# Token operands of the block products formed beside two plain tiles, reloads issued from GpSimd, raw tiles in two rings

## The chip, the cores and the metric

The kernel runs on one core of a Trainium2 chip. A core has a matrix engine (TensorE, PE in the rows), a vector engine (VectorE, DVE), a scalar engine (ScalarE, ACT), GpSimd (POOL) and SyncE (SP). Each runs its own instructions strictly in its own order, and they wait for one another by semaphores. SP and POOL here do little but issue DMAs. The metric is the device time of one launch in microseconds, lower is better.

## The reference

One step of a streaming encoder with two layers over 576 tokens: 512 frames of a new stream and 64 frames of a running one, 2048 features, 16 heads. Each layer is a gated token mixer with a residual. Layer A mixes by chunk-band attention, layer B by latent attention, in which queries come from a low-rank latent `cq` and have a plain part of 128 columns for each head and a rotary part of 64.

```python
def a_prompt(x, ln, w_in, g_q, g_k, table, w_out):
    q, k, v, g = a_project(rmsnorm(x, ln), w_in, g_q, g_k)
...
    y = x + (jax.nn.silu(g) * o) @ w_out

def b_project(h, pos, w_in, g_qa, w_uq, g_kva, g_qn, g_qr, g_kr):
    cq, ckv, kr, g = jnp.split(h @ w_in, [B_Q_RANK, B_Q_RANK + B_KV_RANK, B_Q_RANK + B_KV_RANK + B_ROPE], axis=-1)
    q = (rmsnorm(cq, g_qa) @ w_uq).reshape(b, s, B_HEADS, B_QK)
    q_nope = rmsnorm(q[..., :B_NOPE], g_qn)
    q_rope = rope(rmsnorm(q[..., B_NOPE:], g_qr), pos)
    ckv = rmsnorm(ckv, g_kva)
    k_rope = rope(rmsnorm(kr, g_kr), pos)
    return q_nope, q_rope, ckv, k_rope, g
```

## The kernel before

Features lie on the 128 partitions and the 576 tokens along the free axis, so an activation is 16 tiles of 128x576. Weights and activations are split into a high and a low part, and a product is three matmuls (high x high, low x high, high x low) into the same PSUM tile, in two halves of 288 tokens (`mm3`). The high part is a cast on ACT (L203), the low part a subtraction on DVE (L204); together they are `split`.

The order of the matmuls is written out by a planner, the class behind `od_`: streams of work yield to it, it keeps a clock of its own, and it hands out PSUM tiles of three kinds; the kind `mm`, in which a projection accumulates, has two. PE runs this order and no other. On ACT, DVE, SP and POOL a scheduler sets the order when the kernel is built.

**Output projection, in both layers.** Of the 16 output tiles the first two (m=0, 1) are accumulated beside the last heads of the attention (`both`). Then the scope of the attention closes, and `out_a` or `out_b` runs: the residual is added to m=0 and 1 on DVE (x or by, L833 in layer A and L1222 in layer B), which frees their two `mm` tiles; m=2 and 3 are plain (`proj`, 16 steps of 6 matmuls each); the other twelve go in pairs through `block_pairs`, which makes a pair of outputs from seven half-width products. These need the token operands X of `block_operands`: for each of eight j, four subtractions on DVE and three splits (a cast on ACT and a subtraction on DVE each), on 128x288 halves; they read the gated attention outputs `o[j]` and `o[j + 8]`. In layer A these are still in memory (oA, which the rows name a0sg to a15sg); in layer B they were written to `od` in DRAM, and 16 tiles `bf` are loaded back (L1209). A fourth operand (`last`, boh and bol in layer B) is split after m=3. All of `block_operands` but `last` stands ahead of `out_a` and `out_b` in the program.

**Latents and queries of layer B.** The layer's input comes back from DRAM (`bx`, 16 loads on SP), is scaled and split. Then the latents are projected (cq, kr, ckv), and 24 projections u follow, eight times a rotary tile r and two query tiles q: r0, q0, q1, r1, q2, q3, r2 and so on. Each is accumulated in one `mm` tile and copied by ACT to an SBUF tile called raw (`raw_of`, L478), and the copy frees the `mm` tile. Beside the u the planner lets gates and the other latents through. The chain of a raw tile: square (ACT, L443), cast, sums over the partitions on PE, an inverse root (ACT), scaling on DVE (L474). A query tile is then stored to DRAM by POOL (`qd`, L989), a rotary tile goes through `rope` with four small DMAs on SP and is split (L203, L204), and the key's rotary tile krraw is stored by POOL (`krT`, L945). A tile's memory is free after the last of these. All raw tiles (bx, cqraw, krraw, r, q, ckvraw) come from one pool `latraw` of seven tiles (RAWB), each in the memory of an earlier one that is done.

Of the kernel before, what the change touches and what calls it, by code (L numbers as in the profile page):

```python
# [15 lines left out]
F32 = mybir.dt.float32  # L16
F32R = mybir.dt.float32r
# [101 lines left out]
def encoder(tc, xT, wa_in, wa_out, wb_in, wuq, wuk, wuqr, wuv, wb_out, kcT, vc, ckvcT, krcT, gains, rtab,  # L119
# [128 lines left out]
    def both(pss, name, ws, xs, before):  # L248
# [10 lines left out]
        yield from gens[1]  # L259

    def block_operands(o, o2, pool, name):

        L, R = slice(0, 288), slice(288, 576)
        X = {1: [], 2: [], 3: [], 4: [], 5: [], 6: [], 7: []}
        for j in range(8):  # L270
            X[1].append([x[:, L] for x in o2[j]])
            X[2].append([x[:, L] for x in o2[j + 8]])
            X[3].append([x[:, R] for x in o2[j + 8]])

        def put(p, j, src):
            if p == 4:
                hi, lo = [x[:, R] for x in o2[j]]
            else:
                hi = pool.tile([P, 288], F32R, tag="T", bufs=48, name=f"{name}T{p}h{j}")
                lo = pool.tile([P, 288], F32R, tag="T", bufs=48, name=f"{name}T{p}l{j}")  # L280
            split(src, hi, lo)
            X[p].append((hi, lo))

        sub = ALU.subtract
        for j in range(8):
            a, b = o[j], o[j + 8]
            V.tensor_tensor(out=a[:, L], in0=a[:, R], in1=a[:, L], op=sub)
            put(5, j, a[:, L])
            V.tensor_tensor(out=a[:, R], in0=b[:, R], in1=a[:, R], op=sub)
            V.tensor_tensor(out=b[:, R], in0=b[:, R], in1=a[:, L], op=sub)  # L290
            put(6, j, b[:, R])
            put(7, j, a[:, R])
            V.tensor_tensor(out=b[:, L], in0=b[:, L], in1=b[:, R], op=sub)

        def last():
            for j in range(8):
                put(4, j, o[j + 8][:, L])
        return X, last

# [175 lines left out]

    def raw_of(ps, tp, w, name):
        raw = tp("raw", F32, name)[:, :w]
        ACT.copy(two(raw), ps[:, :, :w // 2])  # L478
        od_.give("mm", L_M)
        return raw  # L480
# [321 lines left out]
    g_T, Tp = pool("blocksa", side="right")  # L802
    X, last_a = block_operands(oA, o2, Tp, "ao")
    g_ao, aop = pool("aout", side="right")
# [18 lines left out]
    def out_a():  # L823
        for m in range(4):
            xr = residual_a(m)
            if m < 2:
                ps = first[m]
            else:
                yield "mm"
                ps = ps_of("mm", f"ao{m}")  # L830
                yield from proj(ps, wo, o2, N)
            x1 = tpo("x1", F32, f"x1_{m}")
            V.tensor_tensor(out=two(x1), in0=ps[:, :, :288], in1=two(xr), op=ALU.add)  # L833
            od_.give("mm", L_M)
            done_a(m, x1)
        last_a()
        yield from block_pairs(wa_out, X, [(m, m + 1) for m in range(4, KT, 2)], raw_a, residual_a,
                               lambda m: tpo("x1", F32, f"x1_{m}"), done_a, "ao")
# [16 lines left out]
    g_l, lp = pool("lat")  # L855
    g_r, lrp = pool("latraw")

    def tpl(tag, dt, name):
        if tag == "raw":
            return lrp.tile([P, N], dt, tag=tag, bufs=RAWB, name=name)  # L860
        bufs = {"s1": SB, "s2": SB, "s3": S3}.get(tag, 1)
        return lp.tile([P, N], dt, tag=tag, bufs=bufs, name=name)

    h = []
    for m in range(KT):
        x1 = tpl("raw", F32, f"bx{m}")
        nc.sync.dma_start(x1, x1d[m * P:(m + 1) * P, :])
        hi = x1p.tile([P, N], F32R, tag="x1", bufs=32, name=f"bh{m}")
        lo = x1p.tile([P, N], F32R, tag="x1", bufs=32, name=f"bl{m}")
        split_g(x1, gn[:, G_LNB + m:G_LNB + m + 1], hi, lo)  # L870
        h.append((hi, lo))
# [34 lines left out]
    def q_latent(m, ps):  # L906
        raw = raw_of(ps, tpl, N, f"cqraw{m}")
        raws.append(raw)
# [14 lines left out]
    def kv_latent(m, ps):  # L923
        raw = raw_of(ps, tpl, N, f"ckvraw{m}")
        raws.append(raw)
# [13 lines left out]
    def rotary_key(ps):  # L939

        raw = raw_of(ps, tpl, N, "krraw")
        st = yield from squares(raw, tpl, N, blk, "kr")
# [41 lines left out]
    def query_chain(hd, ps):  # L984
        n_ = f"q{hd}"
        raw = raw_of(ps, tpl, N, n_ + "raw")
        st = yield from squares(raw, tpl, N, ones, n_)
# [5 lines left out]
    def rotary_chain(pr, ps):  # L993
        n_ = f"r{pr}"
        raw = raw_of(ps, tpl, N, n_ + "raw")
        st = yield from squares(raw, tpl, N, blk, n_)
# [16 lines left out]
    od_.run()  # L1013
    close(g_r)
    close(g_l)
# [189 lines left out]

    oB = []
    for kt in range(KT):
        oB.append(bo.tile([P, N], F32, tag="o", bufs=16, name=f"bf{kt}"))
        nc.sync.dma_start(oB[kt], od[kt * P:(kt + 1) * P, :])  # L1209
    X, last_b = block_operands(oB, o2, bo, "bo")  # L1210

    def out_b():
        for m in range(4):
# [3 lines left out]
            else:  # L1217
                yield "mm"
                ps = ps_of("mm", f"bo{m}")
                yield from proj(ps, wo, o2, N)  # L1220
            y = out_tile_b(m)
# [19 lines left out]
LAHEAD = 1  # L1241
RAWB, SB, S1H, S2H, S3 = 7, 4, 3, 1, 1
S1A, S2A, S3A, L_RS = 3, 2, 1, 5.0
# [83 lines left out]
```

## Time and profile before

| | |
|---|---|
| median of 3 runs | 2041.31 us (2041.11 to 2043.01) |
| profiled execution, its own time | 2043.23 us |
| its span | 2041.5 us |
| mean granted clock of TensorE | 0.991 |
| PE busy | 1990.0 us, 97% |
| DVE busy | 1350.7 us, 66% |
| ACT busy | 1103.4 us, 54% |
| POOL busy | 74.3 us, 4% |

The profile shows one execution. Its own time is 1.7 us more than its span and 1.9 us more than the median. PE is busy in nearly all of the span, so the page is read for the places where PE is idle: the list of its waits, with what released each, then the busy time by stretch, and in a stretch the timelines of the engines. The granted clock is TensorE's, 1.00 for its full speed and 0.50 for half of it.

### The profile page before, as it was taken

The page shows a single profiled execution, that of the slowest core. Times are in us where ns is not written, and L with a number is a line of the kernel's source. Part 1 is how long each engine was busy: PE and PEld are TensorE (multiplying, and loading weights), DVE is VectorE, ACT ScalarE, POOL GpSimd, SP SyncE. Part 2 cuts the span into 40 slices and gives each one's busy share as a digit, 9 for nine tenths or more (in the row PEclk, how much of TensorE's full clock was granted, in tenths as well). Part 3 has the DMA queues.
Part 4 walks back from the last instruction along what each step waited for, and adds up shares of the span by engine and source line. Part 5 has one row for each costly group of instructions (what it writes and reads, how often), then busy time and mean ns, then how long its engine had stood idle before and what let it go on. Part 6 is the DMA issues. An engine that isn't in the chain of part 4 may idle for free.

```text
span 2041.5 us, 37543 instructions
## 1 busy us (share of the span) xinstructions
PE 1990.0 (97%) x14692; PEld 1969.5 (96%) x14692; DVE 1350.7 (66%) x2651; ACT 1103.4 (54%) x2034; POOL 74.3 (4%) x141
## 2 busy tenths in 40 slices
PE   8999999999999999999999899999999999995998
PEld 8999999999999999999999899999999999995998
DVE  7665555555555555558778648887776766676775
ACT  6654444544454445456344538986765656662332
POOL 0000000000000000000000000000000000000000
PEclk9999999999999999999999999999999999997999
DMA  7333333333333333333543535553223322355542
GB/s 210 86 84 94 90 85 90 83 85 89 86 94 89 86 90 78 83 81 101 171 145 118 183 78 147 159 167 112 82 77 98 86 82 84 87 154 196 164 138 68
DMA packets 121393, 223.38 MB, mean 109 GB/s; under 512 B 14272, under 2 KB 29264, under 8 KB 121216
## 3 DMA queue, kind: packets, MB, share of 16 engines
q1 hardware_dynamic: 109360, 181.22, 32.7%
q0 software_dynamic: 11856, 39.76, 5.5%
q8 instruction: 115, 1.88, 0.4%
q14 instruction: 62, 0.51, 0.1%
HBM read 183.92 MB, written 34.36 MB: 107 GB/s over the span
## 4 chain that ended last, share of the span: by engine, by line
PE 85%; issue 8%; DVE 3%; ACT 2%; DMA 1%; POOL 0%; POOLq 0%; SPq 0%; DVEq 0%; ACTq 0%
PE g L164 8%; PE lat L164 6%; PE u L164 3%; PE a2p L164 3%; PE a4p L164 3%; PE a14p L164 3%; PE a12p L164 3%; PE a9p L164 3%; PE a15p L164 3%; PE a11p L164 3%; PE a7p L164 3%; PE a8p L164 3%; PE a5p L164 3%; PE a10p L164 3%; PE a6p L164 3%
## 5 line engine op out<-in xcount | busy, mean ns | idle before, releaser
L204 DVE TENSOR_TENSOR wa_2l<-wa_2r,wa_2h 128x512 fp32r<-128x512 f32 x61 | 42.2, 691 | 92.2 <-ACT wa_2h L203 92.2
L203 ACT CAST wa_2h<-wa_2r 128x512 fp32r<-128x512 f32 x61 | 37.7, 619 | 103.7 <-PE a2p L164 10.1
L204 DVE TENSOR_TENSOR wa_3l<-wa_3r,wa_3h 128x512 fp32r<-128x512 f32 x61 | 42.2, 692 | 44.1 <-ACT wa_3h L203 42.6
L203 ACT CAST wa_0h<-wa_0r 128x512 fp32r<-128x512 f32 x61 | 37.8, 619 | 60.9 <-DMA wa_0r<-wa_in 5.2
L203 ACT CAST wa_3h<-wa_3r 128x512 fp32r<-128x512 f32 x61 | 37.7, 618 | 51.5 <-PE a2p L164 4.5
L204 DVE TENSOR_TENSOR wa_0l<-wa_0r,wa_0h 128x512 fp32r<-128x512 f32 x61 | 41.9, 687 | 17.0 <-ACT wa_0h L203 17.0
L203 ACT CAST wa_1h<-wa_1r 128x512 fp32r<-128x512 f32 x61 | 37.8, 620 | 23.7 <-PE a0pg L164 1.8
L204 DVE TENSOR_TENSOR wa_1l<-wa_1r,wa_1h 128x512 fp32r<-128x512 f32 x61 | 41.8, 685 | 10.5 <-ACT wa_1h L203 10.5
L164 PE MATMUL bo<-boh,wbo_0h 128*128 128x288 f32 x32 | 7.6, 323 | 22.4 <-DVE by L1222 22.4
L164 PE MATMUL u<-cqh,wq_0h 128*128 128x288 f32 x128 | 27.7, 298 | 0.5 <-ACT q6raw L478 0.3
L164 PEld LDWEIGHTS bo<-boh,wbo_0h 128*128 128x128 f32 x32 | 5.8, 214 | 22.6 <-issue 22.6
L164 PE MATMUL u<-cqh,wq_0l 128*128 128x288 f32 x128 | 27.4, 296 | 0.0
L164 PE MATMUL u<-cql,wq_0h 128*128 128x288 f32 x128 | 27.3, 295 | 0.0
L204 DVE TENSOR_TENSOR wb_1l<-wb_1r,wb_1h 128x512 fp32r<-128x512 f32 x25 | 17.2, 687 | 15.2 <-ACT wb_1h L203 15.1
L204 DVE TENSOR_TENSOR wb_3l<-wb_3r,wb_3h 128x512 fp32r<-128x512 f32 x25 | 17.2, 686 | 14.4 <-ACT wb_3h L203 14.3
L203 ACT CAST wb_3h<-wb_3r 128x512 fp32r<-128x512 f32 x25 | 15.4, 616 | 18.1 <-PE lat L164 9.6
L203 ACT CAST wb_1h<-wb_1r 128x512 fp32r<-128x512 f32 x25 | 15.5, 619 | 17.7 <-PE lat L164 8.8
L164 PE MATMUL lat<-bh,wb_0h 128*128 128x288 f32 x88 | 20.0, 311 | 4.5 <-ACT bh L208 4.5
L164 PE MATMUL g<-bh,wb_1h 128*128 128x288 f32 x112 | 24.3, 298 | 0.0
L164 PE MATMUL g<-bh,wb_0h 128*128 128x288 f32 x112 | 24.3, 298 | 0.0
L164 PE MATMUL g<-bh,wb_2h 128*128 128x288 f32 x112 | 24.3, 298 | 0.0
L164 PE MATMUL g<-bh,wb_3h 128*128 128x288 f32 x112 | 24.2, 298 | 0.0
(6782 smaller groups left out, 8051.9 us busy)
## 6 DMA issues: line engine op xcount, KB each, us to landing
wa_0r<-wa_in SPq DMA_DIRECT2D x61, 256.0 KB, 2.9
wa_1r<-wa_in SPq DMA_DIRECT2D x61, 256.0 KB, 2.9
wa_2r<-wa_in SPq DMA_DIRECT2D x61, 256.0 KB, 2.9
wa_3r<-wa_in SPq DMA_DIRECT2D x61, 256.0 KB, 2.9
wb_0r<-wb_in SPq DMA_DIRECT2D x25, 256.0 KB, 2.9
wb_1r<-wb_in SPq DMA_DIRECT2D x25, 256.0 KB, 2.9
wb_2r<-wb_in SPq DMA_DIRECT2D x25, 256.0 KB, 2.9
wb_3r<-wb_in SPq DMA_DIRECT2D x25, 256.0 KB, 2.9
```

The source lines that it names most:

```text
L164: nc.tensor.matmul(out, lhs, rhs, start=start, stop=stop, **kw)
L203: ACT.copy(hi, src)
L204: V.tensor_tensor(out=lo, in0=src, in1=hi.bitcast(F32), op=ALU.subtract)
```

## The change

Three edits. **Forming.** `block_operands` no longer issues its work at the call but returns a generator; `beside` draws one j from it after every fourth step of the plain projections m=2 and m=3, in both layers, so that it now follows the adds of m=0 and 1 in the program. The T tiles are kept by product (T5, T6, T7, 16 each) where one tag had 48. **Reloads.** In layer B the `bf` tiles are loaded in pairs (j and j+8), five pairs ahead, by POOL and no longer by SP; the 16 loads of `bx` go to POOL as well. **Rings.** The pool of seven raw tiles becomes two, of four and of three. The bx tiles go through both; cqraw and ckvraw take the ring of four; krraw and the 24 raw tiles of queries and rotary parts take the ring of three.

```diff
+    def beside(gen, other, n):
+        for j, w in enumerate(gen):
+            yield w
+            if j % n == 0:
+                next(other, None)
     def block_operands(o, o2, pool, name):
...
             else:
-                hi = pool.tile([P, 288], F32R, tag="T", bufs=48, name=f"{name}T{p}h{j}")
-                lo = pool.tile([P, 288], F32R, tag="T", bufs=48, name=f"{name}T{p}l{j}")
+                hi = pool.tile([P, 288], F32R, tag=f"T{p}", bufs=16, name=f"{name}T{p}h{j}")
+                lo = pool.tile([P, 288], F32R, tag=f"T{p}", bufs=16, name=f"{name}T{p}l{j}")
...
-        for j in range(8):
-            a, b = o[j], o[j + 8]
-            V.tensor_tensor(out=a[:, L], in0=a[:, R], in1=a[:, L], op=sub)
-            put(5, j, a[:, L])
...
+        def form():
+            for j in range(8):
+                a, b = o(j)
+                less(a[:, L], a[:, R], a[:, L])
+                put(5, j, a[:, L])
...
+                less(b[:, L], b[:, L], b[:, R])
+                late.append(b[:, L])
+                yield None
...
-        return X, last
+        late = []
+        return X, form(), last
...
-    X, last_a = block_operands(oA, o2, Tp, "ao")
+    X, form_a, last_a = block_operands(lambda j: (oA[j], oA[j + 8]), o2, Tp, "ao")
...
-                yield from proj(ps, wo, o2, N)
+                yield from beside(proj(ps, wo, o2, N), form_a, 4)
...
-    g_r, lrp = pool("latraw")
-
-    def tpl(tag, dt, name):
+    g_r0, lr0 = pool("latraw0")
+    g_r1, lr1 = pool("latraw1")
+    turn = [1, 1, 1, 0, 0, 0, 0]
+
+    def tpl(tag, dt, name, of=None):
         if tag == "raw":
-            return lrp.tile([P, N], dt, tag=tag, bufs=RAWB, name=name)
+            turn.append(turn.pop(0))
+            k = turn[-1] if of is None else of
+            return (lr0, lr1)[k].tile([P, N], dt, tag=tag, bufs=(4, 3)[k], name=name)
...
         x1 = tpl("raw", F32, f"bx{m}")
-        nc.sync.dma_start(x1, x1d[m * P:(m + 1) * P, :])
+        nc.gpsimd.dma_start(x1, x1d[m * P:(m + 1) * P, :])
...
-        raw = raw_of(ps, tpl, N, f"cqraw{m}")
+        raw = raw_of(ps, tpl, N, f"cqraw{m}", of=0)
...
-        raw = raw_of(ps, tpl, N, f"ckvraw{m}")
+        raw = raw_of(ps, tpl, N, f"ckvraw{m}", of=0)
...
-        raw = raw_of(ps, tpl, N, "krraw")
+        raw = raw_of(ps, tpl, N, "krraw", of=1)
...
-        raw = raw_of(ps, tpl, N, n_ + "raw")
+        raw = raw_of(ps, tpl, N, n_ + "raw", of=1)
...
-    oB = []
-    for kt in range(KT):
-        oB.append(bo.tile([P, N], F32, tag="o", bufs=16, name=f"bf{kt}"))
-        nc.sync.dma_start(oB[kt], od[kt * P:(kt + 1) * P, :])
-    X, last_b = block_operands(oB, o2, bo, "bo")
+    def pair_b(j):
+
+        t = []
+        for kt in (j, j + 8):
+            t.append(bo.tile([P, N], F32, tag="o", bufs=16, name=f"bf{kt}"))
+            nc.gpsimd.dma_start(t[-1], od[kt * P:(kt + 1) * P, :])
+        return t
+
+    oB = Ahead((pair_b(j) for j in range(8)), 5)
+    X, form_b, last_b = block_operands(lambda j: oB.get(), o2, bo, "bo")
...
-                yield from proj(ps, wo, o2, N)
+                yield from beside(proj(ps, wo, o2, N), form_b, 4)
```

What it does to the orders is shown at three places. PE's order is the same in both kernels.

ACT in the query stage, around the copy of the rotary tile r2 (r1hi is the cast near the end of r1's chain, q3s the root of q3, wb and wr are weights; the brackets name the semaphores a row waits for, DMASW5_49 and DMASW7_49 being of DMAs that POOL issues). Before:

```order
L203 CAST wb_3h<-wb_3r 128x512 [waits DMAHW5_49,PE_49]
L478 COPY r2raw<-u_14640 128x576 [waits DMASW5_49,PE_49]
L443 ACTIVATE r2sq<-r2raw 128x576 [waits Activation_49]
L203 CAST r2s_14675<-r2sq 128x576 [waits Activation_49]
L203 CAST wr_0h<-wr_0r 128x512 [waits DMAHW6_49,PE_49]
L456 ACTIVATE q3sq<-q3st,epst 128x576 [waits DVE_49,PE_49]
L464 ACTIVATE q3s_14606<-q3sq 128x576 [waits Activation_49]
L466 ACTIVATE q3sq<-q3s_14606 128x576 [waits Activation_49]
L203 CAST r1hi<-r1raw 128x576 [waits DMAHW2_49,DMAHW1_49,DVE_49]
```

After:

```order
L203 CAST wb_3h<-wb_3r 128x512 [waits DMAHW5_49,PE_49]
L203 CAST wr_0h<-wr_0r 128x512 [waits DMAHW6_49,PE_49]
L470 ACTIVATE q3sq<-q3st,epst 128x576 [waits DVE_49,PE_49]
L478 ACTIVATE q3s_14609<-q3sq 128x576 [waits Activation_49]
L480 ACTIVATE q3sq<-q3s_14609 128x576 [waits Activation_49]
L203 CAST r1hi<-r1raw 128x576 [waits DMAHW7_49,DMAHW1_49,DVE_49]
L492 COPY r2raw<-u_14643 128x576 [waits DMASW7_49]
L457 ACTIVATE r2sq<-r2raw 128x576 [waits Activation_49]
L203 CAST r2s_14678<-r2sq 128x576 [waits Activation_49]
```

The copy of r2 stood six rows ahead of the cast of r1, waiting for its matmuls (PE_49) and for a store issued by POOL; now it stands right behind that cast, and waits for a store issued by POOL.

DVE in layer B, where the residual is added to m=0 (by) and m=1. Before:

```order
L204 TENSOR_TENSOR boT7l_22063<-bf_21935,boT7h_22062 128x288
L293 TENSOR_TENSOR bf_21953<-bf_21953 128x288
L204 TENSOR_TENSOR boT5l_22069<-bf_21937,boT5h_22068 128x288
L1222 TENSOR_TENSOR by_22085<-bo_21516,bxr_22083 128x576
L204 TENSOR_TENSOR boT6l_22075<-bf_21953,boT6h_22074 128x288
L1222 TENSOR_TENSOR by_22090<-bo_21523,bxr_22088 128x576
L204 TENSOR_TENSOR boT7l_22079<-bf_21937,boT7h_22078 128x288
```

After:

```order
L204 TENSOR_TENSOR wbo_2l<-wbo_2r,wbo_2h 128x512
L293 TENSOR_TENSOR bf_21952<-bf_21952 128x288
L1246 TENSOR_TENSOR by_21929<-bo_21520,bxr_21927 128x576
L204 TENSOR_TENSOR wbo_3l<-wbo_3r,wbo_3h 128x512
L204 TENSOR_TENSOR boT5l_21978<-bf_21952,boT5h_21977 128x288
L1246 TENSOR_TENSOR by_21934<-bo_21527,bxr_21932 128x576
L293 TENSOR_TENSOR bf_21952<-bf_21954,bf_21952 128x288
L204 TENSOR_TENSOR wbo_0l<-wbo_0r,wbo_0h 128x512
```

The two adds stood behind the forming of all eight j but its last two rows; now the first follows the first subtraction of j=0.

DVE in layer B at the end of the plain tiles: by is the add of m=3 in the rows of after and of m=2 in those of before, bo4p10l the weight that the first block product needs, bol the fourth operand. Before:

```order
L204 TENSOR_TENSOR wbo_2l<-wbo_2r,wbo_2h 128x512
L204 TENSOR_TENSOR wbo_3l<-wbo_3r,wbo_3h 128x512
L1222 TENSOR_TENSOR by_22216<-bo_22095,bxr_22093 128x576
L204 TENSOR_TENSOR bo4p10l<-bo4r_0_22350,bo4p10h 128x512
L204 TENSOR_TENSOR bol_21258<-bf_21939,boh_21257 128x288
L204 TENSOR_TENSOR bol_21288<-bf_21941,boh_21287 128x288
L204 TENSOR_TENSOR bol_21306<-bf_21943,boh_21305 128x288
```

After:

```order
L204 TENSOR_TENSOR bol_21368<-bf_21970,boh_21367 128x288
L204 TENSOR_TENSOR bol_21413<-bf_21974,boh_21412 128x288
L1246 TENSOR_TENSOR by_22328<-bo_22161,bxr_22159 128x576
L204 TENSOR_TENSOR bol_21431<-bf_22024,boh_21430 128x288
L204 TENSOR_TENSOR bol_21453<-bf_22074,boh_21452 128x288
L204 TENSOR_TENSOR bo4p10l<-bo4r_0_22354,bo4p10h 128x512
L204 TENSOR_TENSOR bo4p11l<-bo4r_1_22360,bo4p11h 128x512
```

The weight's split stood behind the add of m=2; now it stands behind the add of m=3 and two rows of the fourth operand.

## Rows read from the trace of the kernel before

**Rows 1.** Waits of PE: what waited <- for what: us in total, times, longest.

```profile
PE bo L164 <- DVE by L1222: 22.4, 1, 22.4
...
PE lat L164 <- ACT bh L208: 4.5, 1, 4.5
PE ao L164 <- DVE x L833: 4.3, 1, 4.3
PE b0t L168 <- DVE b01P L502: 1.3, 1, 1.3
```

**Rows 2.** Windows: busy us (count) of PE, PEld, DVE, ACT, POOL; granted clock; DMA share, GB/s.

```profile
1146.00:1152.00 6.00, 5.84 (x24) 5.49 (x25) 5.43 (x9) 4.09 (x8) 0.00 (x0) 0.53 0.84 259
1220.00:1357.00 137.00, 136.29 (x1018) 135.35 (x1018) 115.97 (x169) 119.66 (x194) 8.13 (x15) 1.00 0.57 155
1852.00:1875.00 23.00, 0.92 (x7) 0.69 (x6) 21.79 (x57) 9.92 (x26) 0.00 (x0) 0.63 0.74 273
```

**Rows 3.** Timeline of DVE at the end of layer B: start, us, instruction, idle before it.

```profile
1851.69 0.46 DVE L287 TENSOR_TENSOR bf<-bf 128x288 f32<-128x288 f32 x1 [4.00 <-DMA bf<-od]
...
1874.47 0.75 DVE L1222 TENSOR_TENSOR by<-bo,bxr 128x576 f32<-128x576 f32 x1
...
1890.56 0.68 DVE L204 TENSOR_TENSOR bo4p10l<-bo4r,bo4p10h 128x512 fp32r<-128x512 f32 x1
```

**Rows 4.** Timelines of POOL and of SP's queue at the end of layer B.

```profile
1845.14 0.54 POOL L1143 DMA_DIRECT2D od<-g15sg  x1 [23.21 <-DVE g15sg L569]
...
1847.36 9.95 SPq L1209 DMA_DIRECT2D bf<-od  x16
```

**Rows 5.** Timeline of PE behind the waits in the two output projections.

```profile
978.37 0.85 PE L164 MATMUL ao<-oh,wao_0h 128*128 128x288 f32 x2 [4.35 <-DVE x L833]
...
984.30 0.45 PE L164 MATMUL ao<-oh,wao_1h 128*128 128x288 f32 x2
...
1878.76 0.42 PE L164 MATMUL bo<-bol,wbo_0h 128*128 128x288 f32 x2
```

**Rows 6.** Timeline of PE behind the first rotary copy of the query stage.

```profile
1242.78 0.53 PE L164 MATMUL u<-cqh,wq_0h 128*128 128x288 f32 x2 [0.18 <-ACT r1raw L478]
```

**Rows 7.** Timeline of ACT in the query stage: copies of raw tiles, one cast.

```profile
1236.77 0.64 ACT L478 COPY q1raw<-u 128x576 f32<-128x576 f32 x1
1242.10 0.63 ACT L478 COPY r1raw<-u 128x576 f32<-128x576 f32 x1
...
1246.80 0.64 ACT L478 COPY q2raw<-u 128x576 f32<-128x576 f32 x1
...
1253.22 0.64 ACT L478 COPY q3raw<-u 128x576 f32<-128x576 f32 x1
...
1258.54 0.63 ACT L478 COPY r2raw<-u 128x576 f32<-128x576 f32 x1
...
1263.36 0.68 ACT L203 CAST r1hi<-r1raw 128x576 fp32r<-128x576 f32 x1
...
1343.72 0.63 ACT L478 COPY r7raw<-u 128x576 f32<-128x576 f32 x1
```

**Rows 8.** Tiles krraw, r1raw, q2raw, q3raw: ns min/median/max, first and last start.

```profile
L945 POOL DMA_DIRECT2D krT<-krraw x1: 549/549/549, 1240.4 to 1240.4; - x1
...
DMA to landing us min/median/max: 2.2/2.5/3.0
...
L204 DVE TENSOR_TENSOR r1lo<-r1raw,r1hi x1: 751/751/751, 1264.7 to 1264.7; 128x576 fp32r<-128x576 f32 x1
...
L989 POOL DMA_DIRECT2D qd<-q2raw x1: 539/539/539, 1261.2 to 1261.2; - x1
...
DMA to landing us min/median/max: 2.4/2.4/2.4
...
L989 POOL DMA_DIRECT2D qd<-q3raw x1: 539/539/539, 1268.0 to 1268.0; - x1
...
DMA to landing us min/median/max: 3.7/3.7/3.7
```

More of the change, by code (lines that the diff above doesn't have):

```diff
@@ L278, in put, with less @@
             else:
-                hi = pool.tile([P, 288], F32R, tag="T", bufs=48, name=f"{name}T{p}h{j}")
-                lo = pool.tile([P, 288], F32R, tag="T", bufs=48, name=f"{name}T{p}l{j}")
+                hi = pool.tile([P, 288], F32R, tag=f"T{p}", bufs=16, name=f"{name}T{p}h{j}")
+                lo = pool.tile([P, 288], F32R, tag=f"T{p}", bufs=16, name=f"{name}T{p}l{j}")
             split(src, hi, lo)
             X[p].append((hi, lo))
-        sub = ALU.subtract
-        for j in range(8):
-            a, b = o[j], o[j + 8]
-            V.tensor_tensor(out=a[:, L], in0=a[:, R], in1=a[:, L], op=sub)
-            put(5, j, a[:, L])
[L289 to L293, printed above, removed]
+        def less(out, a, b):
+            V.tensor_tensor(out=out, in0=a, in1=b, op=ALU.subtract)
+        def form():
[3 more added lines that the diff above has]
+                put(5, j, a[:, L])
+                less(a[:, R], b[:, R], a[:, R])
+                less(b[:, R], b[:, R], a[:, L])
+                put(6, j, b[:, R])
+                put(7, j, a[:, R])
+                less(b[:, L], b[:, L], b[:, R])
+                late.append(b[:, L])
+                yield None
         def last():
             for j in range(8):
-                put(4, j, o[j + 8][:, L])
-        return X, last
+                put(4, j, late[j])
+        late = []
+        return X, form(), last
     def block_weights(w2d, pairs, seq, raw_tile, name):
@@ L474, in scaled, with raw_of @@
         V.scalar_tensor_tensor(out=raw, in0=raw, scalar=col, in1=z, op0=ALU.mult, op1=ALU.mult)
-    def raw_of(ps, tp, w, name):
-        raw = tp("raw", F32, name)[:, :w]
+    def raw_of(ps, tp, w, name, **kw):
+        raw = tp("raw", F32, name, **kw)[:, :w]
         ACT.copy(two(raw), ps[:, :, :w // 2])
@@ L994, in rotary_chain @@
         n_ = f"r{pr}"
-        raw = raw_of(ps, tpl, N, n_ + "raw")
+        raw = raw_of(ps, tpl, N, n_ + "raw", of=1)
         st = yield from squares(raw, tpl, N, blk, n_)
@@ L1013, in encoder @@
     od_.run()
-    close(g_r)
+    close(g_r1)
+    close(g_r0)
     close(g_l)
@@ L1241 @@
 LAHEAD = 1
-RAWB, SB, S1H, S2H, S3 = 7, 4, 3, 1, 1
+SB, S1H, S2H, S3 = 4, 3, 1, 1
 S1A, S2A, S3A, L_RS = 3, 2, 1, 5.0
```

## The prediction

> **What bounds the kernel now.** PE does, nearly everywhere, so the change counts for what it does to PE's idle time and to its clock. I read the list of PE's waits first [rows 1]: 22.4 us for the add by of layer B, 4.5 us at the start of the latents, 4.3 us for the add x of layer A, then 1.3 us. Then the windows [rows 2], for a place where PE has no slack: from 1220 to 1357 us, the query stage, it is busy for 136.29 of 137 us at clock 1.00 (1018 matmuls, 0.134 us each), with ACT busy for 119.66 and DVE for 115.97. Last the timelines of these places, engine by engine.
>
> The change removes two waits of known size, and it shortens the ring through which the whole query stage runs. The first is plainly a gain; the question is what the second costs.
>
> **Layer B's adds, a gain of 24 us.** PE ends m=0 and 1 at 1875.4 − 22.4 = 1853 us (the add ends at 1874.47 + 0.75 = 1875.2 [rows 3], and its matmul starts behind it). In the stretch from 1852 DVE is busy for 21.79 of 23 us, 57 instructions of 0.38 us [rows 2]: the first subtraction starts at 1851.69, when a reload lands, and the add follows the forming [rows 3]. After the change one subtraction stands ahead of it. Its reload is POOL's next DMA behind the store od, which ends at 1845.14 + 0.54 = 1845.7; SP issued the 16 reloads from 1847.36 on [rows 4]. POOL's stores land 2.4 to 3.7 us after their issue [rows 8], so the reload is there at 1848 to 1850, before PE needs the add: the 22.4 us go whole. Behind the wait PE runs at half speed until 1878.76 [rows 5]: 3.4 us for 14 matmuls, which take 14 × 0.134 = 1.9 us at full speed, so 1.5 us more go. Gain 22.4 + 1.5 = 23.9 us.
>
> **What comes in its place.** DVE now forms beside m=2 and 3, which are 192 matmuls or 25.7 us of PE. Its work there is 56 forming instructions (8 × 7), six of the fourth operand and about eleven adds and weight splits of 0.7: 62 × 0.38 + 11 × 0.7 = 31.3 us, less 3 us for a start at 1850. It ends 2.6 us behind PE at worst, near 0 if some weight splits came earlier. Behind the add of m=3 (0.75) two bol (0.38 each) and the split bo4p10l (0.68) [rows 3] now stand ahead of the first block product; before, that split ran at 1890.56, under m=3. Together 2.2 to 4.8 us of a new wait; below nothing is excluded, since that product waited for nothing before. I take 3.
>
> **Layer A's adds, a gain of 7 us.** The wait is 4.35 us, and PE then runs at half speed from 978.37 to 984.30 [rows 5]: 5.9 us for 24 matmuls that take 3.2 us at full speed, 2.7 us lost. In DVE's order the add comes 13 instructions earlier, 13 × 0.38 = 4.9 us, which covers the 4.35. Gain 4.35 + 2.7 = 7.0 us, 3 us at the least if the clock still falls.
>
> **The start of the latents.** bx is loaded by POOL instead of SP. The wait of 4.5 us is for the split of the first loads, and as both queues have nothing ahead of them I count 0, ends −1.5 and +1.5.
>
> **The ring of three, a loss of 31 us.** krraw, r0, q0, q1, r1, q2, q3, r2 and so on now share three tiles, and a copy must wait until the tile whose memory it takes is done: q1 for krraw, an odd q for the odd q before, r2 for q2 and so each r for the even q two before it (in the order above r2's copy waits for a store issued by POOL, and only q tiles have one), q4 for r1. A copy that waits holds its `mm` tile, and PE's next u starts right behind it: behind the copy of r1, which ends at 1242.73 [rows 7], the next u starts at 1242.78 with 0.18 us of wait [rows 6]. So a late copy is a wait of PE at full length, as PE's order has nothing to put in.
>
> q1: krraw's store is issued at 1240.4 and lands up to 3.0 us later [rows 8], 1243.4. The copy was at 1236.77 [rows 7]: 6.6 us late.
>
> r2: q2's store is issued at 1261.2 and lands 2.4 us later [rows 8], 1263.6. The copy was at 1258.54 [rows 7]: 5.1 us late. ACT's own order says much the same: r2's copy stands behind the cast of r1, which starts at 1263.36. This is the upper end, with chains and spacing as before. For the lower end, q2 holds its tile for 1263.6 − 1246.80 = 16.8 us, and its copy can follow that of r1 after one u at the soonest, 24 matmuls or 3.2 us: a period of 20.0 us from r to r, where it was (1343.72 − 1242.10) / 6 = 16.94 us from r1 to r7 [rows 7], 3.1 us late. The other tiles bind less: r1 is held from 1242.10 to 1264.7 + 0.75, 23.4 us, for which its successor q4 has more than a period; q3 from 1253.22 to 1268.0 + 3.7, 18.5 us [rows 7, 8]. Between 3.1 and 5.1 I take 4.0, just below the middle, as an ACT with time left shortens the chains a little. Six periods: 24.0 us, ends 18.6 and 30.6. With q1: 30.6 us, ends 25.2 and 37.2.
>
> **The clock behind these waits.** That is seven waits, one of 6.6 and six of about 4 us. Behind the wait of 4.35 us PE lost 2.7 us at half speed [rows 5], behind that of 4.5 the clock was 0.53 [rows 2]; between 1.3 and 4.3 us the trace has no wait. A slow u also copies its successor later, which the ring passes on. All seven falling costs 7 × 2.7 = 18.9 us, none 0. As the waits stand close to those that let it fall, I take 2.0 each, 14 us.
>
> By a rule of the Trainium skill (TensorE: Matmul & The Clock Gate, HAM oscillation) matmuls that come in bursts with waits between them start every burst slowly, not only the first; the page's example spends 53.3 of 211 us so. By it the last term would be the 18.9 and the time that of the second rival. The rows agree for the waits that they have; none shows one of 4.0 us.
>
> **Sum.** 2043.2 (profiled execution) − 23.9 + 3 − 7.0 + 0 + 30.6 + 14 = 2059.9 us. The median lies 1.9 us below that execution: 2058.0 us. A measurement of this kernel tells about 0.2%, 4 us, from no change.
>
> **Rivals.** First, the clock holds: the waits come out just shorter than 4.3 us, and no u is slowed. For it, the taken value lies below every wait behind which the trace shows a fall; against it, q1's wait is longer. 2041.3 − 27.9 + 30.6 = 2044.0 us.
>
> Second, every wait lets the clock fall, and the chains keep their length. At 4.0 us a period that is 2041.3 − 27.9 + 30.6 + 18.9 = 2062.9 us, at 5.1 it is 2069.5 us. For it, the ACT order that puts the copy behind the cast of r1; against it, the spare time of ACT.
>
> Third, faster: the chains shrink. A hold of 16.8 us in q2 is mostly standing in ACT's and DVE's queues, which are 87 and 85% busy there; if PE waits, these run ahead, and the period may fall to 18 us. The loss is then 6.6 + 2.7 + 6 × 1.1 = 15.9 us with no other fall of the clock: 2041.3 − 27.9 + 15.9 = 2029.3 us. It decides from a period of 16.94 + (27.9 − 9.3) / 6 = 20.0 us downward, at a clock that holds. Against it stand the 20.0 us of the lower end, which only shorter holds undercut, and the order of ACT.
>
> Fourth, POOL's queue is the late one: in layer B the stores of by stand between the reloads, and reloads behind a store wait for its add, so that forming ends later and the first block product waits 8 to 10 us rather than 3, 5 to 7 us more than in the forecast: 2063 to 2065 us. Against it, the adds come at 1853, and 16 reloads took SP 9.95 us [rows 4] of the 25.7.
>
> **How the numbers follow.** Forecast 2058 us (2050 to 2061), chance 0.45; clock holds, 2044, 0.16; all falls, 2063 to 2070, 0.23; shorter chains, 2029, 0.11; POOL's queue, 0.05. The range from 2042 to 2070 leaves out the shorter chains and the tails. Faster 0.11; same 0.10, the greater part of the clock-holds case; slower 0.79.
>
> **What would show it.** PE's list of waits without by, with u waiting for the copies of q1 and r2 to r7, 4 us each and about evenly spaced, at a period near 21 us; the clock of the query stage near 0.9 where it was 1.00; a wait of some 3 us at the first block product. By the Trainium skill (Perfetto Trace Analysis, Optimization Strategy) a gap that repeats on the engine that should be full can mean too little room for the next tile, which is what this ring would look like; no row of before shows one. I am wrong if the copies of r come 18 us apart, or if ACT's copies of r wait for PE.

## The result and the profile after

The change costs time. The median goes from 2042.16 us (of four runs; the 2041.31 given earlier is of three of them) to 2075.38 us; the ratio of after to before is 1.0158, with a 95% interval of 1.0140 to 1.0176. The forecast was 2058 us with a range of 2042 to 2070, so the direction is right and the time lies 5 us above the range.

PE's list of waits after (time, number, longest) answers [rows 1]:

```profile
PE lat L164 <- ACT bh L208: 9.1, 1, 9.1
...
PE u L164 <- ACT q1raw L492: 5.6, 1, 5.6
PE u L164 <- ACT r4raw L492: 5.2, 1, 5.2
PE u L164 <- ACT r6raw L492: 4.8, 1, 4.8
PE bo L164 <- DVE by L1246: 3.9, 1, 3.9
...
PE u L164 <- ACT r2raw L492: 3.6, 1, 3.6
...
PE bo4a L164 <- DVE bo4p10l L204: 2.4, 1, 2.4
PE ao4a L164 <- DVE x L405: 1.9, 1, 1.9
PE bo4c L164 <- ACT bo4p51h L203: 1.5, 1, 1.5
```

The 22.4 us for by have become 3.9 and the wait for x in front of layer A's plain tiles is gone. In their place stand seven waits of u, 29.9 us together (those for r7, r3 and r5, of 3.7, 3.6 and 3.4 us, are left out above), a wait at the latents twice as long as before, a wait of 2.4 us at the first block product of layer B and one of 1.5 us at its second, and a wait of 1.9 us in the block products of layer A, for an add x on DVE. The windows of after (PE, PEld, DVE, ACT, POOL, granted clock, DMA share, GB/s), of the query stage and of the stretch behind the wait for by, against [rows 2]:

```profile
1220.00:1400.00 180.00, 149.67 (x1033) 147.31 (x1032) 120.32 (x171) 123.76 (x198) 8.18 (x15) 0.91 0.44 119
1898.00:1903.00 5.00, 4.21 (x17) 4.22 (x18) 5.00 (x11) 0.87 (x2) 3.42 (x7) 0.50 0.69 175
```

In the query stage PE is idle for 30 of 180 us and runs at a mean clock of 0.91 (it was 1.00). Behind by it still falls to 0.50.

Set side by side, the two profiled executions differ by 31.3 us of span (2041.5 and 2072.8). The places of some instructions, in us from the start:

| place | before | after | shift |
|---|---|---|---|
| last wao_3h matmul of layer A's plain tiles | 1006.0 | 999.4 | −6.6 |
| last matmul of layer A | 1141.1 | 1137.2 | −3.9 |
| first matmul of the latents | 1145.9 | 1146.6 | +0.7 |
| copy of r0 | 1225.6 | 1226.5 | +0.9 |
| copy of r7 | 1343.7 | 1385.2 | +41.5 |
| bol of the last head | 1845.6 | 1887.5 | +41.9 |
| first matmul with bo4p10l | 1902.8 | 1929.7 | +26.9 |
| first matmul with bo14p10l | 2014.1 | 2043.4 | +29.3 |
| end of the span | 2041.5 | 2072.8 | +31.3 |

So the plain tiles of layer A gain 6.6 us. Its block products give 2.7 of them back, 1.9 as the wait for x and the rest at a lower clock behind it (0.91 from 1000 to 1012 us and 0.94 from 1012 to 1024). The start of the latents loses 4.6, the query stage 40.6; the end of layer B gains 15.0; the block products lose 2.4, and the last 2.0 come behind the last matmul, which starts 5.5 us ahead of the end before and 7.5 after.

### The profile page after: what moved, and what is told of

It is laid out like the page before. It is cut to its first block, busy times and chain, and to the rows that moved or that the text cites. A ratio compares the mean times of both kernels' runs of the same rounds, so it can differ in the third digit from the quotient of the medians.

```text
span 2072.8 us, 37566 instructions
## 1 busy us (share of the span) xinstructions
PE 2002.1 (97%) x14692; PEld 1979.3 (95%) x14692; DVE 1353.6 (65%) x2651; ACT 1107.8 (53%) x2034; POOL 91.8 (4%) x173
## 3 DMA queue, kind: packets, MB, share of 16 engines
q1 hardware_dynamic: 104752, 171.78, 30.6%
## 5 line engine op out<-in xcount | busy, mean ns | idle before, releaser
L204 DVE TENSOR_TENSOR wa_0l<-wa_0r,wa_0h 128x512 fp32r<-128x512 f32 x61 | 41.9, 687 | 18.0 <-ACT wa_0h L203 18.0
L204 DVE TENSOR_TENSOR wa_1l<-wa_1r,wa_1h 128x512 fp32r<-128x512 f32 x61 | 41.9, 686 | 11.7 <-ACT wa_1h L203 11.7
L164 PEld LDWEIGHTS u<-cqh,wq_0h 128*128 128x128 f32 x128 | 23.6, 217 | 26.4 <-ACT r4raw L492 5.4
L204 DVE TENSOR_TENSOR wb_2l<-wb_2r,wb_2h 128x512 fp32r<-128x512 f32 x25 | 17.1, 686 | 13.0 <-ACT wb_2h L203 13.0
```

Source lines behind the costliest of these rows:

```text
L164: nc.tensor.matmul(out, lhs, rhs, start=start, stop=stop, **kw)
L204: V.tensor_tensor(out=lo, in0=src, in1=hi.bitcast(F32), op=ALU.subtract)
```

## The experiments

Each kernel was timed in three rounds beside the kernel before on the same chip. Ratios are to that kernel, with the interval of 95%. Its median lay between 2042.16 and 2043.64 us from one set of kernels to the next, so kernels of different sets are compared by their differences from it. The intervals of two ratios leave some 3 us open between two such kernels; where the difference is smaller, the traces are read for it.

**The rings undone.** From the changed kernel:

```diff
-    g_r0, lr0 = pool("latraw0")
-    g_r1, lr1 = pool("latraw1")
+    g_r0, lr0 = pool("latraw")
...
-            return (lr0, lr1)[k].tile([P, N], dt, tag=tag, bufs=(4, 3)[k], name=name)
+            return lr0.tile([P, N], dt, tag=tag, bufs=7, name=name)
```

> The changed kernel with one edit undone: all raw tiles of layer B from one pool of seven again; forming beside the plain tiles and reloads on POOL stay. Theory: the ring of three alone makes the waits of the query stage, in which the trace of the changed kernel is 40.6 us longer (r0 to r7). Then 2075.4 - 40.6 = 2035 us (2032 to 2038), u waits for no copy by over 0.5 us, and the rows of the latents' start and of layer B's end stay as in the changed kernel. Rival: the traffic of POOL's queue slows the query chains (stores qd and krT stand on it); then most of the loss stays, over 2060 us.

Measured 2031.05 us, ratio 0.9938 (0.9923 to 0.9953). PE's waits:

```profile
PE lat L164 <- ACT bh L208: 8.9, 1, 8.9
...
PE bo L164 <- DVE by L1241: 3.0, 1, 3.0
PE bo4a L164 <- DVE bo4p10l L204: 2.5, 1, 2.5
...
PE u L164 <- ACT q6raw L492: 0.3, 1, 0.3
```

No wait of u above 0.3 us is left, the others stay. With the ring undone the rest of the change is 12.6 us faster than the kernel before, where the whole change is 33.2 us slower: 45.8 us hang on the ring, more than the 40.6 us that the trace had shown for the query stage.

**The rings alone**, on the kernel before (in this kernel and in the two with one layer alone the T tiles stay kept by product):

```diff
-    g_r, lrp = pool("latraw")
+    g_r0, lr0 = pool("latraw0")
+    g_r1, lr1 = pool("latraw1")
...
-            return lrp.tile([P, N], dt, tag=tag, bufs=RAWB, name=name)
+            return (lr0, lr1)[k].tile([P, N], dt, tag=tag, bufs=(4, 3)[k], name=name)
```

> The kernel before with the rings of four and three alone; forming and reloads as before. Theory: 2042.2 + 40.6 = 2083 us (2079 to 2087), with seven waits of u for copies of 3 to 6 us each and the wait of 22 us for the add by unchanged. Rival, the rings cost only together with POOL's reloads: under 2060 us.

Measured 2087.13 us, ratio 1.0214 (1.0197 to 1.0231), 43.5 us more than before. The seven waits are those of the changed kernel to 0.1 us, with POOL's queue as before:

```profile
PE u L164 <- ACT q1raw L492: 5.6, 1, 5.6
PE u L164 <- ACT r4raw L492: 5.3, 1, 5.3
...
PE u L164 <- ACT r2raw L492: 3.5, 1, 3.5
```

Undone or done alone, the rings come out at 45.8 and 43.5 us, the same within what the two intervals leave open, so no part of POOL's queue in it is seen.

**One tile more, and one wait less.** Two sizes of the ring, from the changed kernel: four tiles for krraw, r and q (the room comes from three buffers for squares in place of four), and krraw moved to the other ring.

```diff
-    turn = [1, 1, 1, 0, 0, 0, 0]
+    turn = [1, 1, 1, 1, 0, 0, 0, 0]
...
-            return (lr0, lr1)[k].tile([P, N], dt, tag=tag, bufs=(4, 3)[k], name=name)
+            return (lr0, lr1)[k].tile([P, N], dt, tag=tag, bufs=4, name=name)
...
-SB, S1H, S2H, S3 = 4, 3, 1, 1
+SB, S1H, S2H, S3 = 3, 3, 1, 1
```

> The changed kernel with one tile more in the ring of krraw, r and q (four and four; three buffers for squares where there were four make the room). Theory: the three holds of 23, 17 and 18.5 us need 58.7 / 4 = 14.7 us per period in four tiles, less than PE's 16.9, so no copy waits by over 1.5 us and the time is that of the kernel with seven, 2031 to 2036 us. Rival, a ring apart from the other latents is bad at any size: over 2050 us.

Measured 2032.89 us, ratio 0.9954 (0.9939 to 0.9969), 9.9 us less than the kernel before: within 3 us of seven shared tiles, and the intervals overlap. One wait of 1.6 us is left, for r1, and none for r2 to r7.

```diff
-        raw = raw_of(ps, tpl, N, "krraw", of=1)
+        raw = raw_of(ps, tpl, N, "krraw", of=0)
```

> The changed kernel with krraw alone moved to the ring of four. Theory: the waits of the query stage add up one by one; q1's wait of 5.6 us and the slow stretch of 2.7 us behind it go, the six waits of r stay: 2075.4 - 8.3, 2066 to 2068 us. Rival: the ring as a whole sets the pace, and the next copies wait by what q1 no longer does: 2073 to 2076 us.

Measured 2069.26 us, ratio 1.0138 (1.0121 to 1.0155), 26.5 us more than the kernel before and so 6.7 less than the changed kernel, a little above the expected 2066 to 2068:

```profile
PE u L164 <- ACT r4raw L492: 5.2, 1, 5.2
PE u L164 <- ACT r6raw L492: 4.8, 1, 4.8
PE u L164 <- ACT r2raw L492: 4.3, 1, 4.3
```

q1 waits no more, and of the other six only r2 grew, from 3.6 to 4.3 us; but new small waits came, 1.7 us for r1, 1.0 for ckvraw and 0.4 for q3. From the copy of r0 to that of r7 the trace is 155.5 us long, 3.2 less than the 158.7 of the changed kernel and not the 8.3 expected. The other 5.3 us that this trace gains up to r7 lie ahead of the first latent matmul (1141.3, not 1146.6), where the edit was not aimed, and the profiled execution is the fastest of its four. So the waits do not simply add up: 3.8 of the 5.6 us that q1 no longer waits come back at its neighbours, and the rival has its share.

**Layer A alone.** The kernel before, with forming beside the plain tiles in layer A:

```diff
-                yield from proj(ps, wo, o2, N)
+                yield from beside(proj(ps, wo, o2, N), form_a, 4)
```

> The kernel before with forming beside the plain tiles in layer A alone; bx on SP, one pool of seven, layer B as before. Theory: in the changed kernel the 7 us of layer A were given back at the latents because the cast of krc stands ahead of the first bh on ACT and waits for a late DMA; with bx on SP that cast stands behind the first bh, so some of the gain lasts: 2042.2 - 3 to - 7, 2035 to 2039 us. Rival: the start of the latents is held by something that the projection does not move (the norm's sum, the reload of x); then the wait of PE there grows by all that the add gained, 2042 us.

Measured 2034.45 us, ratio 0.9955 (0.9940 to 0.9970), 9.2 us less: the whole gain lasts. (2.1 us of it are a shorter wait for by, 20.3 us in place of 22.4, which this edit was not aimed at; with the rings alone it is 20.8.) Its first latent matmul comes at 1138.9 us, 7.0 us earlier than before, and the wait there is 4.5 us as before. So the start of the latents follows layer A, if bx is on SP. What holds it in the changed kernel stands on ACT (timeline: start, us, instruction, idle before it):

```profile
1145.53 0.30 ACT L203 CAST KRh<-krc 128x128 fp32r<-128x128 f32 x1 [5.28 <-DMA krc<-krcT]
1145.74 2.10 ACT L208 ACTIVATE bh<-bx,gn 128x576 fp32r<-128x576 f32 x3
...
L966 SPq DMA_DIRECT2D krc<-krcT x1: 424/424/424, 1137.6 to 1137.6; - x1
DMA to landing us min/median/max: 7.9/7.9/7.9
```

The cast of krc, a 64 KB load of the cached rotary keys, stands ahead of the first bh and waits 5.3 us for its load, which SP issues at 1137.6 and which takes 7.9 us. In the kernel before it takes 3.7 us, and its cast stands behind the first bh:

```profile
1145.08 0.77 ACT L208 ACTIVATE bh<-bx,gn 128x576 fp32r<-128x576 f32 x1
1145.76 0.28 ACT L203 CAST KRh<-krc 128x128 fp32r<-128x128 f32 x1
...
DMA to landing us min/median/max: 3.7/3.7/3.7
```

**Whether krc or bx holds the latents.** From the kernel with seven raw tiles (bx on POOL), krc moved to POOL, behind sin:

```diff
-        nc.sync.dma_start(cc, krcT)
+        nc.gpsimd.dma_start(cc, krcT)
```

> The changed kernel with one pool of seven raw tiles, bx on POOL as changed, and only the small load krc moved to POOL behind sin, by which its cast falls behind the second bh on ACT. Theory: what held the latents was that cast in front of the first bh, waiting for a load that took 7.9 us; then bh starts some 4 us earlier and the time is 2031 - 4 to - 5, 2026 to 2027 us. Rival: the loads bx by POOL are late themselves: 2031 us, with the first bh waiting for its bx.

Measured 2032.88 us, ratio 0.9952 (0.9937 to 0.9967): 10.0 us less than the kernel before, where seven tiles alone gave 12.6: no gain, and not for the rival's reason. Two bh start at 1138.99, so bx was there, and then the cast stops ACT again:

```profile
1138.99 1.44 ACT L208 ACTIVATE bh<-bx,gn 128x576 fp32r<-128x576 f32 x2
1145.33 0.30 ACT L203 CAST KRh<-krc 128x128 fp32r<-128x128 f32 x1 [4.89 <-DMA krc<-krcT]
...
DMA to landing us min/median/max: 7.1/7.1/7.1
```

Then krc with memory of its own, issued ahead of the first bx:

```diff
+    g_k, kp = pool("krcp")
+    krc = kp.tile([P, NC], F32, name="krc")
+    nc.gpsimd.dma_start(krc, krcT)
     h = []
...
-        cc = lp.tile([P, NC], F32, tag="cc", bufs=1, name="krc")
-        nc.sync.dma_start(cc, krcT)
-        split(cc, KR[0][:, :NC], KR[1][:, :NC])
+        split(krc, KR[0][:, :NC], KR[1][:, :NC])
```

> The changed kernel with one pool of seven raw tiles and bx on POOL, and the small load krc given memory of its own and issued by POOL ahead of the first bx, some 12 us before its cast is due. Theory: the latents start late for the load krc alone, which falls into the burst of POOL's and SP's loads behind layer A and lands 7 to 8 us after its issue; with krc out of the way the first latent follows layer A's last matmul after 5 us, not 9.5: 2031 - 4 to - 5, 2026 to 2027 us. Rival: the first bx by POOL are late themselves and hold bh: 2031 us.

Measured 2027.21 us, ratio 0.9927 (0.9912 to 0.9941), 15.6 us less than the kernel before and 3.0 less than with seven tiles alone, which the two intervals do not tell apart. The trace does: the first latent matmul follows layer A's last by 7.2 us, not by 9.2. PE waits 6.9 us at the latents where it was 8.9, and no longer for krc:

```profile
1135.16 0.29 ACT L203 CAST KRh<-krc 128x128 fp32r<-128x128 f32 x1
...
1140.59 0.30 ACT L203 CAST ckvh<-cc 128x128 fp32r<-128x128 f32 x1 [3.04 <-DMA cc<-ckvcT]
...
DMA to landing us min/median/max: 3.8/3.8/3.8
```

The load now lands in 3.8 us and its cast is out of the way, but the next small load, cc of the cached latents, has taken its place ahead of the first bh. The two had shared one buffer: with krc out of it, SP issues the first cc at 1134.8, where it had come at 1143.6, behind the split of krc. So my theory was half right: it is not krc alone, but whichever small load has its cast in front of bh while it lands late.

**bx back on SP**, with forming in both layers, POOL's bf and seven tiles:

```diff
-        nc.gpsimd.dma_start(x1, x1d[m * P:(m + 1) * P, :])
+        nc.sync.dma_start(x1, x1d[m * P:(m + 1) * P, :])
```

> The changed kernel with one pool of seven raw tiles and with bx loaded on SP as before; forming beside the plain tiles in both layers and POOL's reloads of bf stay. Theory: with bx on POOL the latents start 9.5 us after layer A's last matmul, with bx on SP 5.1, so 4 to 5 us come back against 2031 us, and one us at the end of the program from 16 fewer DMAs of POOL: 2024 to 2026 us; the sum of the two runs with one layer each would be 2043.6 - 9.2 - 13.2 = 2021 us. Rival: POOL's bx is not what holds the latents: 2031 us.

Measured 2024.42 us, ratio 0.9909 (0.9892 to 0.9925), 18.5 us less than the kernel before and 5.9 less than with bx on POOL. The first latent matmul follows layer A's last by 4.8 us again (1134.6 and 1139.4), as in the kernel before; with bx on POOL it is 9.2 (1134.8 and 1144.0). These 4.4 us and 1.3 at the end of the program, which is treated below, are the difference.

**Layer B alone.** The kernel before, with forming beside the plain tiles and POOL's bf in layer B:

```diff
-    oB = []
-    for kt in range(KT):
-        oB.append(bo.tile([P, N], F32, tag="o", bufs=16, name=f"bf{kt}"))
-        nc.sync.dma_start(oB[kt], od[kt * P:(kt + 1) * P, :])
+    oB = Ahead((pair_b(j) for j in range(8)), 5)
...
-                yield from proj(ps, wo, o2, N)
+                yield from beside(proj(ps, wo, o2, N), form_b, 4)
```

> The kernel before with forming beside the plain tiles and POOL's reloads in layer B alone; layer A, bx and the pool of seven as before. Theory: the end of layer B is worth what the trace of the changed kernel shows behind the attention, 42.0 - 31.3 = 10.7 us less: 2031.5 us (2029 to 2034), with a wait of some 4 us for the add by, released by the reload of the residual bxr. Rival, the sum of the prediction (the wait goes whole, 3 us come at the first block product): 20.9 us less, 2021 us.

Measured 2030.48 us, ratio 0.9932 (0.9917 to 0.9947), 13.2 us less than the kernel before, near what the trace gave and far from the 20.9 of the prediction. In the changed kernel, DVE waits for the add like this, with the DMAs behind it (SP's queue, then POOL):

```profile
1890.87 0.46 DVE L293 TENSOR_TENSOR bf<-bf 128x288 f32<-128x288 f32 x1 [1.24 <-DMA bf<-od]
1897.97 0.76 DVE L1246 TENSOR_TENSOR by<-bo,bxr 128x576 f32<-128x576 f32 x1 [6.64 <-DMA bxr<-x1d]
...
1888.91 0.33 SPq L217 DMA_DIRECT2D wbo_0r<-wb_out  x1
1889.29 0.91 SPq L1216 DMA_DIRECT2D bxr<-x1d  x2
...
1887.62 2.66 POOL L1230 DMA_DIRECT2D bf<-od  x5
...
DMA to landing us min/median/max: 2.7/3.4/8.8
```

The reload bf is not late: the first subtraction runs at 1890.87, before PE ends m=1 at 1894.9. DVE then stands idle for 6.64 us, until the residual bxr lands, which SP issues at 1889.29, behind a weight load that waits for DVE, and the slowest bxr lands 8.8 us after its issue, beside five reloads of POOL. The kernel with layer B alone shows the same wait of DVE, 7.13 us for bxr.

**The residual out of the way.** From the kernel with bx on SP: the two bxr of m=0 and 1 issued by POOL ahead of bf; and, in a second kernel, issued by SP ahead of bf with bf on SP too.

```diff
+    early = [residual_b(m, nc.gpsimd) for m in range(2)]
     oB = Ahead((pair_b(j) for j in range(8)), 5)
...
-            xr = residual_b(m)
+            xr = early.pop(0) if early else residual_b(m)
```

> As the kernel with both layers formed beside, bx on SP and seven raw tiles, and the two residual reloads bxr of m=0 and 1 issued by POOL ahead of the reloads bf, not by SP behind a weight load. Theory: the add by waits for bxr, which SP issues late and which lands 8.6 us later beside five bf; with it gone the wait of 3 to 4.5 us and the slow stretch of 2.7 us behind it go: 5 to 7 us below the kernel with bx on SP, 2016 to 2020 us. Rival: the bf reloads themselves come late, then the first subtraction takes the place of bxr and the time stays within 2 us.

Measured 2021.74 us, ratio 0.9898 (0.9883 to 0.9913), 2.7 us less than with bx on SP where I expected 5 to 7. The wait for by is gone, but the one behind it grew from 2.4 to 5.6 us:

```profile
PE bo4a L164 <- DVE bo4p10l L204: 5.6, 1, 5.6
...
1873.27 1.56 DVE L204 TENSOR_TENSOR bol<-bf,boh 128x288 fp32r<-128x288 f32 x4
1874.74 0.76 DVE L1242 TENSOR_TENSOR by<-bo,bxr 128x576 f32<-128x576 f32 x1
...
1876.51 0.69 DVE L204 TENSOR_TENSOR bo4p10l<-bo4r,bo4p10h 128x512 fp32r<-128x512 f32 x1
```

From 1855 us on DVE is busy without a gap, through the forming, eight bol and the add to bo4p10l. It has become the bound of the plain tiles: what PE gains in front of them it waits for behind them.

```diff
-            nc.gpsimd.dma_start(t[-1], od[kt * P:(kt + 1) * P, :])
+            nc.sync.dma_start(t[-1], od[kt * P:(kt + 1) * P, :])
```

> As the kernel with both layers formed beside, bx on SP and seven raw tiles, but with the bf reloads on SP too. In SP's order 13 of them stand ahead of the weight load wbo_1r of m=2, which PE needs some 3 us after it starts. Theory: 16 loads took SP 10 us, so PE waits some 5 us for that weight, and the time is 4 to 8 us above the kernel with bf on POOL: 2028 to 2033 us. Rival: nothing of m=2 waits for SP and the queue of the reloads is worth nothing: within 2 us of it.

Measured 2020.77 us, ratio 0.9893 (0.9878 to 0.9908). I was wrong and the rival right: POOL's queue is worth nothing for bf, as the 1.0 us to the kernel above is the shorter end of the program (5.5 us behind the last matmul in place of 6.4). PE does not wait for the weight load, which is further ahead than I took it to be.

**The fourth operand later.** From the last kernel, in both layers (layer B's lines are shown):

```diff
-        last_b()
-        yield from block_pairs(wb_out, X, [(m, m + 1) for m in range(4, KT, 2)], raw_b, residual_b, out_tile_b,
-                               done_b, "bo")
+        yield from after_some(last_b, block_pairs(wb_out, X, [(m, m + 1) for m in range(4, KT, 2)], raw_b,
+                               residual_b, out_tile_b, done_b, "bo"))
```

where after_some calls it behind the eighth step of the block products.

> As the kernel with both layers formed beside, seven raw tiles and all reloads on SP, with the fourth operand (the eight bol and boh, and their like in layer A) split behind the first matmuls of the first block product and not ahead of it. Theory: in the 4.4 us that PE waits there for bo4p10l, DVE works off eight bol at 0.37 us; 3 us of it go: 2017 to 2019 us. Rival: DVE is late with the forming itself; then the wait moves to the next products and the time stays at 2020 to 2021 us.

Measured 2017.18 us, ratio 0.9876 (0.9862 to 0.9891), 3.5 us less than the kernel before it in this list, the fastest of all and as expected. The wait of 4.4 us is gone; 1.4 us come at the second weight of the next product:

```profile
PE bo4c L164 <- ACT bo4p51h L203: 1.4, 1, 1.4
...
PE bo4a L164 <- ACT bo4p61h L203: 0.7, 1, 0.7
```

## Why the prediction was right in direction and short in time

**The ring of three** was the decisive term, and its size came out. Its seven waits were put at 30.6 us and measure 29.9, q1 at 6.6 (5.6), the mean of the six of r at 4.0 (4.1). The mechanism shows in ACT's copies, against [rows 7]:

```profile
1250.51 0.63 ACT L492 COPY r1raw<-u 128x576 f32<-128x576 f32 x1
...
1272.49 0.63 ACT L492 COPY r2raw<-u 128x576 f32<-128x576 f32 x1
...
1316.22 0.64 ACT L492 COPY r4raw<-u 128x576 f32<-128x576 f32 x1 [2.27 <-DMA qd<-q6raw]
...
1362.05 0.64 ACT L492 COPY r6raw<-u 128x576 f32<-128x576 f32 x1 [0.82 <-DVE r5lo L204]
```

r2 comes 22.0 us after r1, and r4's copy waits for the store qd of q6, as foreseen; its wait is the longest of r because that store took 4.1 us to land, where those of the other even q took 2.4 to 2.6. The copies of r2, r3, r5 and r7 start within 0.4 us of the landing of the even q's store, too. Only r6 goes otherwise: it waits for r5lo, the last use of r5, and starts before the store of q10 has landed (issued at 1360.4, 2.4 us to landing). The mean period from r1 to r7 is (1385.2 − 1250.5) / 6 = 22.5 us, more than the 20.9 of 16.94 + 4.0, since the slow stretches add to it. The reason given for taking 4.0 and not 5.1 did not show: the chains did not shrink, the even q that an r waits for held their tiles for 16.1 to 17.4 us where it was 16.8 for q2. That the mean came out is in part luck. With four tiles the waits of r2 to r7 and of q1 are gone; with krraw out of the ring q1's wait is gone, but not for its full price.

**The clock behind the waits** was put at 14 us and is 10.6, counted as the prediction counted it (from the first matmul behind a wait until full speed, less 0.134 us for each): 1.8 us behind q1, then 1.4, 0.1, 1.7, 1.6, 2.6 and 1.4 behind r2 to r7. All but one of the seven waits let the clock fall, for 12 to 24 matmuls, where the two waits of [rows 5] gave 24 and 14. Two waits of nearly one length went differently (timeline of PE: start, us, the wait in brackets; a row of two matmuls takes 0.68 us and more at half speed, 0.42 at full):

```profile
1273.17 0.85 PE L164 MATMUL u<-cqh,wq_0h 128*128 128x288 f32 x2 [3.60 <-ACT r2raw L492]
1273.82 0.68 PE L164 MATMUL u<-cql,wq_0h 128*128 128x288 f32 x2
...
1295.11 0.53 PE L164 MATMUL u<-cqh,wq_0h 128*128 128x288 f32 x2 [3.56 <-ACT r3raw L492]
1295.47 0.42 PE L164 MATMUL u<-cql,wq_0h 128*128 128x288 f32 x2
```

From the copy of r0 to the last head of layer B the changed kernel loses 41.0 us (41.9 − 0.9 in the table), and waits and clock are 40.5 of them; the forecast was 44.6.

So the query stage came out 4 us cheaper than forecast. The time lies above the range because of four other terms.

**The start of the latents** failed first, by 4.6 us. I counted bx on POOL at 0 us, with the reason that both queues have nothing ahead of the first loads. That reason looked at bx alone. The edit also moved, in the orders of SP and ACT, the load krc and its cast, and it moved loads in time: SP had issued seven bx from 1120.7 to 1132.4, well ahead of krc at 1139.8, while POOL issues the last two of its seven from 1135.7 to 1136.7, within 2 us of krc at 1137.6. krc lands in 7.8 us with bx on POOL and seven tiles, in 4.0 with bx on SP and forming in layer A, in 3.8 when issued early. That bx on POOL costs these 4 us at the latents is shown by moving it back. That krc lands late because the bytes of other loads go first is not shown by an edit; it is inferred from what moves while it is in flight (windows of before and after, as [rows 2]):

```profile
1139.80:1143.50 3.70, 1.56 (x12) 1.33 (x11) 1.59 (x3) 0.72 (x2) 1.61 (x3) 1.00 0.87 262
1137.60:1145.50 7.90, 0.00 (x0) 0.00 (x0) 2.59 (x4) 1.81 (x3) 1.08 (x2) 0.63 0.92 295
```

The DMA engines are nearly as busy in both, but at 262 GB/s for 3.7 us some 1.0 MB pass before krc has landed, and at 295 GB/s for 7.9 us some 2.3 MB.

**Layer A** gained at the plain tiles what was foreseen (7.0 us, 6.6 measured), and with bx on SP all of it reaches the end. But the prediction costed the wait that forming puts in front of the block products for layer B alone; for layer A it was left at nothing, and 2.7 us went there, 1.9 of them the wait for an add x of a DVE that is busy for 10.9 of the 12 us from 1000. This wait differs between kernels with the same layer A, from 0.3 to 2.4 us.

**Layer B's end** was 6 us short: 20.9 foreseen (23.9 less 3), 15.0 measured. The failed step is "the 22.4 us go whole": the prediction followed the subtraction that stands ahead of the add in DVE's order, with its reload bf, and not the add's own operand, the residual bxr. The rows before could not show a wait for it, since the forming hid it, but the trace of before had its issue, on SP's queue behind the 16 bf:

```profile
1857.79 1.09 SPq L1197 DMA_DIRECT2D bxr<-x1d  x2
```

That is 5 us after PE ended m=1 at 1853, so as the queue stood the add could not have followed at once. In the changed kernel the 16 bf are off that queue and bxr is issued at 1889.29, 5.6 us before PE ends m=1 at 1894.9, but the slowest of its loads lands 8.8 us later. The clock then fell behind 3.9 us too, for 24 matmuls and not 14, so the 1.5 us of the slow stretch did not go but became 2.5. With 18.5 us less of waiting, 1.0 more of slow clock and the 2.4 us of the new wait the sum is 15.1. The new wait at the first block product looks right (3 foreseen, 2.4 measured), but that is luck: it is short because the add comes late. Where bxr is on time and the wait for by is gone, as the sum supposed, it is 5.6 and 4.4 us, around the upper end of 4.8. The 2.4 us in the block products, 1.7 of them waits at the second product, were not foreseen.

**The end of the program**, 2.0 us, had no term at all.

Of the rivals, the clock that holds, the chains that shrink and the late queue of POOL at the block products did not come. The second, each wait with its slow stretch and chains of full length, has the nearest time (2063 to 2070 us), but not by its sum: it wants 18.9 us of slow clock where there are 10.6, and the query stage cost less than even the forecast. Its nearness is luck as well.

## What to carry to other kernels

A gain at a wait is worth what the next thing due allows: list all operands of the instruction that becomes first, each with the queue that loads it, and then ask the same of the next stage. A ring of buffers is costed from the trace as copy to last use of each tile, stores included, against the period of the producer; one tile too few here cost some 45 us, where the rest of the change gained 12.6. An edit of a queue can act through a small load of another tile that merely shares the time.

## What the runs showed of the hardware

- The time between the start of the last matmul and the end of the span grows with the number of POOL's instructions, nearly all DMAs: 5.5 us with 141 (before, and the fastest kernel), 6.3 with 157 (layer B alone), 7.5 with 173 (changed, and with seven tiles). That is 0.06 us each on average. Why was not tried.
- The granted clock fell to 0.50 behind waits as short as 2.5 us: with seven tiles, 19 matmuls go at half speed behind the 2.54 us for bo4p10l, the first of them 1 us after PE had started again; in the changed kernel it stayed at 1.00 behind the 2.35 us there.
- The same load of 64 KB lands in 3.6 to 4.0 us or in 6.4 to 7.9 us. While it is in flight the DMA engines move about 1.0 MB in the first case (before, bx on SP, krc issued early) and 2.0 to 2.5 MB in the second (changed, seven tiles, krraw moved, krc on POOL), on either queue.
